# Branch B of a hybrid encoder layer: half of the weights' lower parts and the fourths' sums move to GpSimd, PSUM banks come from three pools, two steps begin later

## The chip, the cores and the metric

The kernel runs on one core of a Trainium2 chip, with TensorE (PE, with its weight loads PEld), VectorE (DVE), ScalarE (ACT), GpSimd (POOL) and SyncE (SP). The metric is the device time of one execution in microseconds (us); lower is better. Every time is of the whole kernel unless a part is named.

## The reference, cut to what matters

One layer, 512 tokens, D = 2048, float32. Both branches and the merge; the change touches branch B and the start of the product with w_out.

```python
h = rmsnorm(x, g_pre)
qkv, z_a, b_raw, a_raw, glu_in, z_b, gate_logits = split(h @ w_in)
y_a = (rmsnorm(gated_delta(conv4(qkv))) * silu(z_a)) @ w_br_a          # branch A
u = causal_depthwise_conv(glu(glu_in), w_dw) + b_dw                    # branch B, 31 taps
u = silu(layernorm(u, ln_g, ln_b)) * silu(z_b)
y_b = u @ w_br_b
gate_a, gate_b = split(sigmoid(gate_logits + b_gate))
x = x + rmsnorm((gate_a * y_a + gate_b * y_b) @ w_out, g_post)
x = x + rmsnorm(sigmoid(x @ w_ple_gate) * (p @ w_ple_proj), g_ple)
```

## The kernel before

**Precision.** A float32 product is made of three matmuls on parts of shorter mantissa: x = xh + xl, w = wh + wl, and x w is xh wh + xl wh + xh wl. Each weight block of 128 x 512 is loaded (two blocks in one transfer, `raw`), its higher part `w[:, 0:T]` is a cast on ScalarE (L126), its lower part a subtraction raw - higher (L127) on the engine that `low_part[0]` names, VectorE at first. The two parts lie in a ring of four buffers `w`; `next_piece()` keeps up to three blocks prepared ahead. A block serves six matmuls in branch B (two row blocks t, three each).

**Order of the work.** A deque `jobs` holds the products in order. Each matmul calls `tick()`, which lets side generators (the normalisation `norm`, `mix`) run on between the matmuls; a `yield n` there waits n ticks. A scheduler then fixes an order for each engine; `pin(...)` keeps an instruction at the place where it was issued. So each engine works through a fixed queue, and an instruction that waits holds up all behind it.

**Normalisation of branch B** (`layer_norm`, L1187 to L1263), while branch A's last products run: load the 16 blocks `ur`; the sum over the channels by a matmul with ones (`sum_ps`, L1200) from `acc`, which GpSimd accumulates (L977); subtract the mean (L1207), squares (L1209, ScalarE) and their sum (L1211, VectorE); reciprocal root `rst` on GpSimd (L1219), spread by a matmul into `rstd_ps` (L1227, PSUM); then per block times rstd (L1231, one input in PSUM), silu (ScalarE), times silu(z_b) (L1236), and the split into higher and lower part `uh`, `ul` (L1245 to L1248).

**Branch B's product** (L1370 to L1497) is done by a Winograd-like scheme on quarters: seven products on sums of quarters for each column half jp (0, 1). The sums of the activations are S1 to S4 (L1262, each on 128 x 256 in float32, then split by `sw_split`: cast on ScalarE, `opl` on VectorE, L1305); S4 takes up S2's buffers. The sums of the weights were made before and lie in memory. In the order of the jobs: P1, P2, Q4 for both column halves (96 matmuls each), then for each half Q5, P6, P7, P3 (48 each). A product's results lie in four (or two) PSUM banks from `b_bank()`, always of the pool `yps` with four banks; branch A's end uses the same pool, and `gt<-yp` (L1158) empties it there. After a product come VectorE's combinations: `snap_b` copies (L1429, ScalarE), `tt_b` sums and differences (L1433), and `fin_b`, which multiplies by the gate (L1291) and adds to `mixed` = `gt` (L1294). P7 ends two column blocks and P2 and P3 one, so a burst of 15 VectorE operations follows P7 of the first half (jp 0), two of them reading PSUM (`yp`).

**From branch B to w_out.** `mix` (`split_mixed`) turns the finished `mixed` by transposes on TensorE (`turned`, `tp`, L1318) and makes the operands of the next product, also in quarters: `combine_low` for the first half of the columns, `combine_high` (four steps, with splits and sums on VectorE, L1305, L1349 to L1357) for the other. It runs beside P3 and the second half. The product with w_out begins with P1, P7, P1, P7; its weights are blocks of 128 x 1024 (`wsp`, higher part L1553, lower part L1554 on VectorE); its banks `f` come from `bank()`: two of `ups`, four of `fps`, two of `gps`, and round again.

Of the kernel before, what the change touches and what calls it, by code (L numbers as in the profile page):

```python
# [81 lines left out]
def _body(ctx, tc, A, out):  # L82
# [28 lines left out]

    prep_src = deque()
    prepped = deque()
    low_part = [nc.vector]

    def prep():
        if not prep_src:
            return
        src = prep_src.popleft()
        raw = rawp.tile([P, 1024], F32, tag="raw", name="raw", bufs=3)  # L120
        nc.sync.dma_start(raw, src)
        for q in range(2):
            rq = raw[:, q * T:(q + 1) * T]
            w = ring.tile([P, 1024], F32R, tag="w", name="w")
            hi, lo = w[:, 0:T], w[:, T:]
            nc.scalar.copy(hi, rq)  # L126
            low_part[0].tensor_tensor(lo, rq, hi.bitcast(F32), ALU.subtract)  # L127
            hi_lo[id(hi)] = w.rearrange("p (s c) -> p s c", s=2)
            prepped.append((hi, lo))

# [29 lines left out]
    def run_jobs():  # L160
        while jobs:
            jobs.popleft()()
# [833 lines left out]
    def convs():  # L996
        ready = last = None
        while scanning[0] < NH // 2 - 1:
            yield 4
        while len(done) < NK:  # L1000
            ready = ready or near()
            if not ready:
                if last and len(taken) == NK:
                    filtered(*last)
                    last = None
                yield 1
                continue
            (i, u, y), ready = ready, None
            w0 = V_DW + i * TAPS
            for s in range(1, TAPS):  # L1010
                pin(nc.vector.scalar_tensor_tensor(y[:, s:], u[:, 0:T - s], vv(w0 + TAPS - 1 - s), y[:, s:], ALU.mult, ALU.add))  # L1011
                if s == 28 and last:
                    filtered(*last)
                    last = None
                if s == 24:
                    ready = near()
                yield pace(s)
            nc.sync.dma_start(u_dram[i], y)
            last = i, y
            if ups and not taken_ps[0]:  # L1020
                taken_ps[0] = True
                low_part[0] = nc.gpsimd

    def side_convs():
        for _ in range(SIDE):
# [161 lines left out]
    def hp(name):  # L1187
        return hpool.tile([P, T], F32, tag="h", name=name)

    def layer_norm():  # L1190
        for i in range(NK):
            while i not in done:
                yield
            u_t[i] = hp("ur")
            nc.sync.dma_start(u_t[i], u_dram[i])
            yield 1
        low_part[0] = nc.vector
        yield 8
        pm = ups.tile([P, T], F32, tag="u", name="sum_ps")
        pin(mm(pm, ones, acc[0], start=True, stop=True))  # L1200
        mean = ups.tile([P, T], F32, tag="u", name="mean_ps")
        nc.scalar.activation(mean, pm, AF.Copy, scale=1.0 / D)
        acc2 = hp("acc2")
        yield 6
        for i in range(NK):
            u = u_t[i]
            pin(nc.vector.tensor_tensor(u, u, mean, ALU.subtract))  # L1207
            sq = hp("lsq") if i else acc2
            nc.scalar.activation(sq, u, AF.Square)  # L1209
            if i:  # L1210
                pin(nc.vector.tensor_tensor(acc2, acc2, sq, ALU.add))  # L1211
            yield 7
        pvr = ups.tile([P, T], F32, tag="u", name="var_ps")
        for tt in range(NTT):
            mm(pvr[:, tt:tt + 1], acc2[:, tt * P:(tt + 1) * P], ones[:, 0:1], start=True, stop=True)
        var = lnp.tile([P, NTT], F32, name="var")
        nc.vector.tensor_scalar(var, pvr[:, 0:NTT], 1.0 / D, EPS, ALU.mult, ALU.add)
        rst = lnp.tile([P, NTT], F32, name="rst")
        nc.gpsimd.tensor_tensor(rst, var, mhalf_c[:, 0:NTT], ALU.pow)  # L1219
        dg = hp("dg")  # L1220
        for tt in range(NTT):
            nc.vector.tensor_scalar(dg[:, tt * P:(tt + 1) * P], ident, rst[:, tt:tt + 1], None, ALU.mult)
        for i in range(3):
            load_zb(i)
        yield 22
        rstd = ups.tile([P, T], F32, tag="u", name="rstd_ps")
        pin(mm(rstd, ones, dg, start=True, stop=True))  # L1227
        yield 6
        for i in range(NK):
            u = u_t[i]  # L1230
            pin(nc.vector.tensor_tensor(u, u, rstd, ALU.mult))  # L1231
            nc.scalar.activation(u, u, AF.Silu, scale=vv(V_LNG + i), bias=vv(V_LNB + i))
            yield 6
            if i + 3 < NK:
                load_zb(i + 3)
            nc.vector.tensor_tensor(u, u, zb[i], ALU.mult)  # L1236
            if i < 8:
                if i % 2 == 0:
                    ua[i // 2] = low(0, "uh"), low(0, "ul")
                c = slice((i % 2) * 256, (i % 2) * 256 + 256)  # L1240
                uh, ul = [x[:, c] for x in ua[i // 2]]
                nc.scalar.copy(uh, u[:, LO])
                nc.vector.tensor_tensor(ul, u[:, LO], uh.bitcast(F32), ALU.subtract)
            else:
                uh, ul = low(0, "uh"), low(LOP if i == NK - 1 else 0, "ul")  # L1245
                nc.scalar.copy(uh, u)
                nc.vector.tensor_tensor(ul, u, uh.bitcast(F32), ALU.subtract)
            uT[i] = (uh, ul)  # L1248
            yield 6
        us1, us3 = [None] * 4, [None] * 4  # L1250
        for name in ("S1", "S2", "S3", "S4"):
            for k2 in range(4):
                if name == "S1":
                    us1[k2] = hp("usf")
                elif name == "S3":
                    us3[k2] = hp("usf")
                t = us3[k2] if name == "S3" else us1[k2]
                for kk, c in halves(k2):
                    u, v = u_t[kk], u_t[kk + 8]
                    a, b, op = {"S1": (u[:, HI], v[:, HI], ALU.subtract), "S2": (t[:, c], u[:, LO], ALU.subtract),  # L1260
                                "S3": (u[:, LO], u[:, HI], ALU.subtract), "S4": (t[:, c], v[:, LO], ALU.add)}[name]
                    nc.vector.tensor_tensor(t[:, c], a, b, op)  # L1262
                yield 4  # L1263
                uS[name][k2] = sw_split(*((s2, "s2") if name == "S1" else (hpool, "h") if name == "S3" else (lop, "lop")), t)
                yield 6

    def load_zb(i):
        zb[i] = hp("zb")
# [45 lines left out]
    def turned(kk):  # L1314
        ps = gps.tile([P, T], F32, tag="g", name="tp")
        for tt in range(NTT):
            c = (kk % 4) * P
            nc.tensor.transpose(ps[:, tt * P:(tt + 1) * P], mixed[tt][kk // 4][:, c:c + P], ident)  # L1318
        return ps

    def combine_low(k2):
        while added[k2 // 2] < NTT:
            yield
        ah = hpool.tile([P, T], F32R, tag="h", name="ah")
        al = hpool.tile([P, T], F32R, tag="h", name="al")
        s3_ = hpool.tile([P, T], F32, tag="h", name="sf")
        for kk, c in halves(k2):
            ps = turned(kk)
            yield 2
            cm[kk] = slots.tile([P, T], F32, tag="s", name="cm")  # L1330
            nc.scalar.copy(cm[kk], ps)
            nc.scalar.copy(ah[:, c], cm[kk][:, LO])
            nc.vector.tensor_tensor(al[:, c], cm[kk][:, LO], ah[:, c].bitcast(F32), ALU.subtract)
            nc.vector.tensor_tensor(s3_[:, c], cm[kk][:, LO], cm[kk][:, HI], ALU.subtract)
            yield
        AW["A11"][k2] = (ah, al)
        Sf[k2] = s3_

    def combine_high(k2):
        while added[k2 // 2 + 2] < NTT:  # L1340
            yield
        two = [turned(kk + 8) for kk, _ in halves(k2)]
        yield 2
# [46 lines left out]
        return [x[:, c:c + P] for x in uS[name][kk // 2]]  # L1390

    b_banks = [0]

    def b_bank():
        b_banks[0] += 1
        return yps.tile([P, T], F32, tag="y", name="yp")

    def b_job(products, done_, gates=()):
# [37 lines left out]
    def branch_b():  # L1436
# [40 lines left out]
        b_job([(0, "P1"), (1, "P1")], p1, [(S2_, LOW, 0), (S2_, LOW, 2)])  # L1477
        b_job([(0, "P2"), (1, "P2")], p2)
        b_job([(0, "Q4"), (1, "Q4")], q4)
        jobs.append(lambda: finish("norm"))  # L1480
        for jp in range(2):
            b_job([(jp, "Q5")], q5(jp))
            b_job([(jp, "P6")], p6(jp), [(LO_, HIGH, 2 * jp + 1), (LO_, HIGH, 2 * jp)])
# [7 lines left out]
    lnp_ctx = ExitStack()  # L1491
    lnp = lnp_ctx.enter_context(tc.tile_pool(name="lnp", bufs=1))
    run_jobs()
    lnp_ctx.close()
    s2_ctx.close()

# [77 lines left out]
            mm(ps, lh, wl[:, c], start=False, stop=kk == 7)  # L1574

    banks = [-1]

    def bank():
        banks[0] += 1
        if banks[0] % 8 < 2:  # L1580
            return ups.tile([P, T], F32, tag="u", name="f")
        if banks[0] % 8 < 6:
            return fps.tile([P, T], F32, tag="f", name="f")
        return gps.tile([P, T], F32, tag="g", name="f")

# [313 lines left out]
```

## Time and profile before

| | us |
|---|---|
| median of 3 runs | 2441.02 (2440.77 to 2441.69) |
| the profiled execution | 2441.21 |
| its span | 2439.4 |
| TensorE busy | 2399.4 |
| VectorE busy | 1877.9 |
| ScalarE busy | 1206.9 |
| GpSimd busy | 496.5 |

Times in the trace count from the span's start; the profiled execution takes 1.8 us more than its span. The normalisation's mean falls at about 1833 (L1200), its reciprocal root at 1869 (L1227), P1 begins at about 1900, P7 of the first half ends near 2014, the product with w_out begins near 2091. A row of the timeline is: start, time of the row, engine, line, operation, out<-in, shapes, x how many; in brackets the idle time before it and what ended that. Several like instructions in a run make one row, and since instructions overlap at their ends, n of them take less than n times the time of one.

### The profile page before, as it was taken

How to read it: one execution, taken by the hardware profiler on the slowest of the kernel's cores; microseconds unless marked ns; L12 is line 12 of the kernel's file. 1: busy time of each engine (PE TensorE's matmuls, PEld its weight loads, DVE VectorE, ACT ScalarE, POOL GpSimd, SP SyncE). 2: the span in 40 equal slices, each digit the busy share in tenths (PEclk: the TensorE clock that was granted, in tenths of full speed). 3: DMA queues.
4: the chain of work that ended last, by engine and by line, in shares of the span. 5: the costliest groups of instructions: out<-in, count | busy, mean ns of one | idle time of the engine just before them, and what ended most of it. 6: DMA issues, size and time to landing. Idle time of an engine off the chain costs nothing. (4 is left out here: it accounts for less than half of the span.)

```text
span 2439.4 us, 33786 instructions
## 1 busy us (share of the span) xinstructions
PE 2399.4 (98%) x11870; PEld 1972.0 (81%) x11870; DVE 1877.9 (77%) x3500; ACT 1206.9 (49%) x2409; POOL 496.5 (20%) x513
## 2 busy tenths in 40 slices
PE   9999999999999999999999999999999899999998
PEld 7888888887788888888888887888887687787886
DVE  8878878776778677776868778999998868867644
ACT  6455545554554545445454544544325554644532
POOL 1001110011112112111212213998730000000000
PEclk9999999999999999999999999999999999999999
DMA  7576776664366565556565453533534465764652
GB/s 273 171 201 189 212 200 206 202 164 167 131 173 185 165 186 144 189 151 173 153 193 173 130 170 94 160 128 105 179 116 164 147 207 182 258 204 146 211 175 76
DMA packets 142234, 417.96 MB, mean 171 GB/s; under 512 B 16240, under 2 KB 24688, under 8 KB 141040
## 3 DMA queue, kind: packets, MB, share of 16 engines
q1 hardware_dynamic: 120304, 327.71, 39.8%
q0 software_dynamic: 19456, 83.90, 14.9%
q10 hardware_dynamic: 2304, 4.20, 0.5%
q8 instruction: 93, 1.52, 0.2%
q14 instruction: 77, 0.63, 0.1%
HBM read 384.28 MB, written 98.57 MB: 198 GB/s over the span
## 5 line engine op out<-in xcount | busy, mean ns | idle before, releaser
L126 ACT CAST w<-raw 128x512 fp32r<-128x512 f32 x628 | 385.9, 618 | 495.9 <-PE g L187 261.5
L185 PE MATMUL g<-hl,w 128*128 128x512 f32 x1536 | 610.5, 397 | 0.0
L187 PE MATMUL g<-hh,w 128*128 128x512 f32 x1536 | 608.2, 396 | 0.0
L183 PE MATMUL g<-hh,w 128*128 128x512 f32 x1536 | 608.1, 396 | 0.0
L127 DVE TENSOR_TENSOR w<-raw,w 128x512 fp32r<-128x512 f32 x514 | 355.1, 698 | 148.6 <-ACT w L126 146.3
L185 PEld LDWEIGHTS g<-hl,w 128*128 128x128 f32 x1536 | 289.0, 188 | 55.4 <-issue 1.4
L183 PEld LDWEIGHTS g<-hh,w 128*128 128x128 f32 x1536 | 289.2, 188 | 54.1
L187 PEld LDWEIGHTS g<-hh,w 128*128 128x128 f32 x1536 | 289.1, 188 | 54.0 <-POOL w L127 0.3
L1011 DVE SCALAR_TENSOR_TENSOR uc<-up,vec,uc 128x497 f32<-128x497 f32 (+29 forms) x390 | 282.3, 734 | 13.2 <-ACT uc L990 1.9
L127 POOL TENSOR_TENSOR w<-raw,w 128x512 fp32r<-128x512 f32 x114 | 146.6, 1299 | 58.0 <-ACT w L126 57.6
L710 DVE SCALAR_TENSOR_TENSOR cv<-g,vec,cv 128x511 f32<-128x511 f32 x144 | 106.6, 740 | 41.1 <-ACT cv L708 40.8
L1149 PE MATMUL yp<-w,oh 128*128 128x512 f32 x256 | 100.1, 391 | 0.0
L1151 PE MATMUL yp<-w,ol 128*128 128x512 f32 x256 | 99.5, 391 | 0.0
L1147 PE MATMUL yp<-w,oh 128*128 128x512 f32 x256 | 99.1, 389 | 0.0
L898 DVE TENSOR_TENSOR prod<-UT,VT 128x2 f32<-128x2 f32 (+30 forms) x248 | 87.2, 352 | 6.5
L1516 POOL TENSOR_TENSOR rmsm<-totm,mhalf_c 128x2 f32<-128x2 f32 x2 | 2.1, 1040 | 386.2 <-DVE totm L1514 386.2
L1033 POOL TENSOR_TENSOR uc<-uc,pr 128x511 f32<-128x511 f32 (+29 forms) x60 | 75.9, 1265 | 8.3 <-ACT pr L1032 7.7
L1748 PE MATMUL f<-w,xh 128*128 128x512 f32 x192 | 75.1, 393 | 1.0 <-DVE xl L1669 1.0
L1749 PE MATMUL f<-w,xh 128*128 128x512 f32 x192 | 75.1, 391 | 0.3 <-DVE w L127 0.3
L1573 PE MATMUL f<-wsp,opl 128*128 128x512 f32 x192 | 75.3, 392 | 0.0
L1572 PE MATMUL f<-wsp,oph 128*128 128x512 f32 x192 | 75.1, 391 | 0.0
L1750 PE MATMUL f<-w,xl 128*128 128x512 f32 x192 | 74.9, 390 | 0.0
(424 smaller groups left out, 5029.9 us busy)
## 6 DMA issues: line engine op xcount, KB each, us to landing
raw<-in_w_in SPq DMA_DIRECT2D x194, 512.0 KB, 3.4
wb_sums<-in_w_br_b POOLq DMA_DIRECT2D x48, 512.0 KB, 7.3
wo_sums<-in_w_out POOLq DMA_DIRECT2D x48, 512.0 KB, 8.0
raw<-in_w_ple_gate SPq DMA_DIRECT2D x40, 512.0 KB, 4.0
raw<-in_w_br_a SPq DMA_DIRECT2D x32, 512.0 KB, 3.4
raw<-wb_sums SPq DMA_DIRECT2D x32, 512.0 KB, 3.9
raw<-in_w_ga SPq DMA_DIRECT2D x24, 512.0 KB, 4.8
raw<-in_w_gb SPq DMA_DIRECT2D x24, 512.0 KB, 4.8
```

Of the source, the lines that this page charges most:

```text
L126: nc.scalar.copy(hi, rq)
L127: low_part[0].tensor_tensor(lo, rq, hi.bitcast(F32), ALU.subtract)
L183: mm(ps, wh, rh, start=(k == 0), stop=False)
L185: mm(ps, wh, rl, start=False, stop=False)
L187: mm(ps, wl, rh, start=False, stop=(k == NK - 1))
L710: nc.vector.scalar_tensor_tensor(y[:, s:], ps[:, 0:T - s], vv(w0 + 3 - s), y[:, s:], ALU.mult, ALU.add)
L898: pin(nc.vector.tensor_tensor(pv_, um, vm, ALU.mult))
L1011: pin(nc.vector.scalar_tensor_tensor(y[:, s:], u[:, 0:T - s], vv(w0 + TAPS - 1 - s), y[:, s:], ALU.mult, ALU.add))
L1033: pin(nc.gpsimd.tensor_tensor(y[:, s:], y[:, s:], pr[:, s:], ALU.add))
L1147: mm(ps[tt], lh[:, b], wh, start=k == 0, stop=False)
L1149: mm(ps[tt], lh[:, b], wl, start=False, stop=False)
L1151: mm(ps[tt], ll[:, b], wh, start=False, stop=k == NK - 1)
```

## The change

- `low_part` becomes a list of two, for the two blocks of a transfer. In the convolution's time both are GpSimd, as before. The normalisation no longer gives them back to VectorE at its start but in its mean loop at i = 11; after `rst` the first of the two goes to GpSimd again, to the end of branch B. So from `rst` on every second lower part is made on GpSimd (60 of 120).
- The sums S1 to S4 (32 operations on 128 x 256) move from VectorE to GpSimd, with 7 and 7 ticks behind each instead of 4 and 6; S4 begins only when Q4 is done; the call that finished the normalisation ahead of Q5 is gone.
- `b_bank()`: of the products, counted by `b_banks // 2` (two banks each), number 0 and 4 (P1 and Q4 of the first half) take their banks from `gps`, 3, 7 and 10 (P2 of the second half, P6 of the first, Q5 of the second) from `ups`, the others from `yps`.
- The first transpose of each `turned` is pinned. `combine_low` waits 24 ticks before its first block; `combine_high` does not begin until branch B's jobs have all run (`ending`).
- The final stage's banks come in another order: `ffffuuffuuffffgg`, then round by eights.

The lines move a little: L1219 becomes L1220, L1231 L1233, L1262 L1266, L1291 and L1294 L1295 and L1298, L1305 L1309, L1318 L1322, L1433 L1447, L1554 L1569.

GpSimd's order from the reciprocal root on. Before, it holds nothing more of branch B after it; `rmsm` belongs to the norm after w_out:

```order
L977 TENSOR_TENSOR acc<-acc,uc 128x512
L127 TENSOR_TENSOR w<-raw,w 128x512 x7
L977 TENSOR_TENSOR acc<-acc,uc 128x512 x2
L1219 TENSOR_TENSOR rst<-var,mhalf_c 128x4
L1516 TENSOR_TENSOR rmsm_20387<-totm_20384,mhalf_c 128x2
```

Now (`w` is a lower part, `usf` a sum of quarters, its inputs `ur` the normalised blocks):

```order
L977 TENSOR_TENSOR acc<-acc,uc 128x512
L127 TENSOR_TENSOR w<-raw,w 128x512 x5
L1220 TENSOR_TENSOR rst<-var,mhalf_c 128x4
L127 TENSOR_TENSOR w<-raw,w 128x512 x3
L1266 TENSOR_TENSOR usf<-ur 128x256
L127 TENSOR_TENSOR w<-raw,w 128x512
L1266 TENSOR_TENSOR usf<-ur 128x256 x2
L127 TENSOR_TENSOR w<-raw,w 128x512
L1266 TENSOR_TENSOR usf<-ur 128x256 x3
L127 TENSOR_TENSOR w<-raw,w 128x512
L1266 TENSOR_TENSOR usf<-ur 128x256 x3
L127 TENSOR_TENSOR w<-raw,w 128x512
```

So lower parts and sums stand in turn in a queue that was empty; 60 lower parts and 32 sums follow `rst`, and lower parts stand ahead of the last accumulation of the mean (L977) as of `rst` itself.

VectorE's order at the end of P7 of the first half. Before (`bsnap` are the copies of earlier products, `bd` a difference kept for P3, `gt` the mixed rows):

```order
L127 TENSOR_TENSOR w<-raw,w 128x512 x8
L1433 TENSOR_TENSOR bsnap<-yp,bsnap 128x512
L127 TENSOR_TENSOR w<-raw,w 128x512
L1433 TENSOR_TENSOR bsnap<-bsnap 128x512 x2
L1291 TENSOR_TENSOR bsnap<-bsnap,gb 128x512 x2
L1433 TENSOR_TENSOR bd<-bsnap 128x512
L1294 TENSOR_TENSOR gt<-gt,bsnap 128x512
L1433 TENSOR_TENSOR bsnap<-yp,bsnap 128x512
L1294 TENSOR_TENSOR gt<-gt,bsnap 128x512
L1433 TENSOR_TENSOR bsnap<-bsnap 128x512 x2
L1291 TENSOR_TENSOR bsnap<-bsnap,gb 128x512 x2
L1294 TENSOR_TENSOR gt<-gt,bsnap 128x512 x2
```

and now:

```order
L127 TENSOR_TENSOR w<-raw,w 128x512 x4
L1447 TENSOR_TENSOR bsnap<-yp,bsnap 128x512
L1447 TENSOR_TENSOR bsnap<-bsnap 128x512 x2
L1295 TENSOR_TENSOR bsnap<-bsnap,gb 128x512 x2
L1447 TENSOR_TENSOR bd<-bsnap 128x512
L1298 TENSOR_TENSOR gt<-gt,bsnap 128x512
L1447 TENSOR_TENSOR bsnap<-yp,bsnap 128x512
L1298 TENSOR_TENSOR gt<-gt,bsnap 128x512
L1447 TENSOR_TENSOR bsnap<-bsnap 128x512 x2
L1295 TENSOR_TENSOR bsnap<-bsnap,gb 128x512 x2
L1298 TENSOR_TENSOR gt<-gt,bsnap 128x512 x2
L127 TENSOR_TENSOR w<-raw,w 128x512 x4
```

The 15 operations are the same, but no lower part of VectorE's stands among them any more, and half as many stand ahead of them, since the others are in GpSimd's queue.

VectorE's order where the last stage opens, before (`wsp` are lower parts of w_out's blocks, `opl`, `sf` the splits and sums of `combine_high`, `bd` P3's end):

```order
L1305 TENSOR_TENSOR opl<-tp,oph 128x512 x2
L127 TENSOR_TENSOR w<-raw,w 128x512
L1349 TENSOR_TENSOR sf<-cm,tp 128x256 x2
L127 TENSOR_TENSOR w<-raw,w 128x512 x2
L1305 TENSOR_TENSOR opl<-sf,oph 128x512
L1554 TENSOR_TENSOR wsp<-raw,wsp 128x1024
L1353 TENSOR_TENSOR sf<-sf,cm 128x256 x2
L1433 TENSOR_TENSOR bd<-yp,bd 128x512 x2
```

and now:

```order
L127 TENSOR_TENSOR w<-raw,w 128x512 x3
L1569 TENSOR_TENSOR wsp<-raw,wsp 128x1024
L1447 TENSOR_TENSOR bd<-yp,bd 128x512 x2
L1295 TENSOR_TENSOR bd<-bd,gb 128x512 x2
L1298 TENSOR_TENSOR gt<-gt,bd 128x512 x2
L1569 TENSOR_TENSOR wsp<-raw,wsp 128x1024 x2
L1309 TENSOR_TENSOR opl<-sf,oph 128x512 x3
L1569 TENSOR_TENSOR wsp<-rw,wsp 128x1024
```

Here the whole of `combine_high` has moved behind P3's end, and three `wsp` come ahead of its first operation on VectorE (its splits of `tp` come later still).

```diff
@@ -111,7 +111,7 @@
 
     prep_src = deque()
     prepped = deque()
-    low_part = [nc.vector]
+    low_part = [nc.vector, nc.vector]
 
     def prep():
         if not prep_src:
@@ -124,7 +124,7 @@
             w = ring.tile([P, 1024], F32R, tag="w", name="w")
             hi, lo = w[:, 0:T], w[:, T:]
             nc.scalar.copy(hi, rq)
-            low_part[0].tensor_tensor(lo, rq, hi.bitcast(F32), ALU.subtract)
+            low_part[q].tensor_tensor(lo, rq, hi.bitcast(F32), ALU.subtract)
             hi_lo[id(hi)] = w.rearrange("p (s c) -> p s c", s=2)
             prepped.append((hi, lo))
 
@@ -1019,7 +1019,7 @@
             last = i, y
             if ups and not taken_ps[0]:
                 taken_ps[0] = True
-                low_part[0] = nc.gpsimd
+                low_part[:] = [nc.gpsimd] * 2
 
     def side_convs():
         for _ in range(SIDE):
@@ -1194,7 +1194,6 @@
             u_t[i] = hp("ur")
             nc.sync.dma_start(u_t[i], u_dram[i])
             yield 1
-        low_part[0] = nc.vector
         yield 8
         pm = ups.tile([P, T], F32, tag="u", name="sum_ps")
         pin(mm(pm, ones, acc[0], start=True, stop=True))
@@ -1209,6 +1208,8 @@
             nc.scalar.activation(sq, u, AF.Square)
             if i:
                 pin(nc.vector.tensor_tensor(acc2, acc2, sq, ALU.add))
+            if i == 11:
+                low_part[:] = [nc.vector] * 2
             yield 7
         pvr = ups.tile([P, T], F32, tag="u", name="var_ps")
         for tt in range(NTT):
@@ -1217,6 +1218,7 @@
         nc.vector.tensor_scalar(var, pvr[:, 0:NTT], 1.0 / D, EPS, ALU.mult, ALU.add)
         rst = lnp.tile([P, NTT], F32, name="rst")
         nc.gpsimd.tensor_tensor(rst, var, mhalf_c[:, 0:NTT], ALU.pow)
+        low_part[0] = nc.gpsimd
         dg = hp("dg")
         for tt in range(NTT):
             nc.vector.tensor_scalar(dg[:, tt * P:(tt + 1) * P], ident, rst[:, tt:tt + 1], None, ALU.mult)
@@ -1249,6 +1251,8 @@
             yield 6
         us1, us3 = [None] * 4, [None] * 4
         for name in ("S1", "S2", "S3", "S4"):
+            while name == "S4" and not b_u[0].get("s4"):
+                yield 4
             for k2 in range(4):
                 if name == "S1":
                     us1[k2] = hp("usf")
@@ -1259,10 +1263,10 @@
                     u, v = u_t[kk], u_t[kk + 8]
                     a, b, op = {"S1": (u[:, HI], v[:, HI], ALU.subtract), "S2": (t[:, c], u[:, LO], ALU.subtract),
                                 "S3": (u[:, LO], u[:, HI], ALU.subtract), "S4": (t[:, c], v[:, LO], ALU.add)}[name]
-                    nc.vector.tensor_tensor(t[:, c], a, b, op)
-                yield 4
+                    nc.gpsimd.tensor_tensor(t[:, c], a, b, op)
+                yield 7
                 uS[name][k2] = sw_split(*((s2, "s2") if name == "S1" else (hpool, "h") if name == "S3" else (lop, "lop")), t)
-                yield 6
+                yield 7
 
     def load_zb(i):
         zb[i] = hp("zb")
@@ -1315,12 +1319,16 @@
         ps = gps.tile([P, T], F32, tag="g", name="tp")
         for tt in range(NTT):
             c = (kk % 4) * P
-            nc.tensor.transpose(ps[:, tt * P:(tt + 1) * P], mixed[tt][kk // 4][:, c:c + P], ident)
+            turn = nc.tensor.transpose(ps[:, tt * P:(tt + 1) * P], mixed[tt][kk // 4][:, c:c + P], ident)
+            if tt == 0:
+                pin(turn)
         return ps
 
     def combine_low(k2):
         while added[k2 // 2] < NTT:
             yield
+        if k2 == 0:
+            yield 24
         ah = hpool.tile([P, T], F32R, tag="h", name="ah")
         al = hpool.tile([P, T], F32R, tag="h", name="al")
         s3_ = hpool.tile([P, T], F32, tag="h", name="sf")
@@ -1337,7 +1345,7 @@
         Sf[k2] = s3_
 
     def combine_high(k2):
-        while added[k2 // 2 + 2] < NTT:
+        while not ending:
             yield
         two = [turned(kk + 8) for kk, _ in halves(k2)]
         yield 2
@@ -1390,9 +1398,15 @@
         return [x[:, c:c + P] for x in uS[name][kk // 2]]
 
     b_banks = [0]
+    ending = []
 
     def b_bank():
+        n = b_banks[0] // 2
         b_banks[0] += 1
+        if n in (3, 7, 10):
+            return ups.tile([P, T], F32, tag="u", name="yp")
+        if n in (0, 4):
+            return gps.tile([P, T], F32, tag="g", name="yp")
         return yps.tile([P, T], F32, tag="y", name="yp")
 
     def b_job(products, done_, gates=()):
@@ -1477,7 +1491,6 @@
         b_job([(0, "P1"), (1, "P1")], p1, [(S2_, LOW, 0), (S2_, LOW, 2)])
         b_job([(0, "P2"), (1, "P2")], p2)
         b_job([(0, "Q4"), (1, "Q4")], q4)
-        jobs.append(lambda: finish("norm"))
         for jp in range(2):
             b_job([(jp, "Q5")], q5(jp))
             b_job([(jp, "P6")], p6(jp), [(LO_, HIGH, 2 * jp + 1), (LO_, HIGH, 2 * jp)])
@@ -1491,6 +1504,8 @@
     lnp_ctx = ExitStack()
     lnp = lnp_ctx.enter_context(tc.tile_pool(name="lnp", bufs=1))
     run_jobs()
+    ending.append(True)
+    low_part[:] = [nc.vector] * 2
     lnp_ctx.close()
     s2_ctx.close()
 
@@ -1574,12 +1589,15 @@
             mm(ps, lh, wl[:, c], start=False, stop=kk == 7)
 
     banks = [-1]
+    order = "ffffuuffuuffffgg"
 
     def bank():
         banks[0] += 1
-        if banks[0] % 8 < 2:
+        n = banks[0]
+        kind = order[n] if n < 16 else order[8 + n % 8]
+        if kind == "u":
             return ups.tile([P, T], F32, tag="u", name="f")
-        if banks[0] % 8 < 6:
+        if kind == "f":
             return fps.tile([P, T], F32, tag="f", name="f")
         return gps.tile([P, T], F32, tag="g", name="f")
 
```

## The prediction

> **What bounds the kernel now.** I read the page's head first, then the windows around branch B, then the waits of TensorE there.
>
> ```profile
> span 2439.4 us, 33786 instructions
> PE 2399.4 (98%) x11870; PEld 1972.0 (81%) x11870; DVE 1877.9 (77%) x3500; ACT 1206.9 (49%) x2409; POOL 496.5 (20%) x513
> ```
>
> TensorE is busy 98% of the span, so the kernel ends when TensorE's work ends, and the change can only win or lose what TensorE idles (or runs at a lower clock) in the stretch that it touches. The windows show where that is; the columns are busy time of PE, PEld, DVE, ACT and POOL, each with its instructions, then the granted clock and the DMA.
>
> ```profile
> core 0: us, PE busy (x) PEld busy (x) DVE busy (x) ACT busy (x) POOL busy (x), PEclk, DMA share, GB/s
> 1800.00:1860.00 60.00, 59.57 (x261) 48.65 (x260) 50.06 (x79) 21.51 (x37) 7.72 (x6) 1.00 0.32 106
> 1860.00:1885.00 25.00, 24.22 (x108) 19.28 (x107) 20.55 (x39) 14.35 (x24) 1.04 (x1) 1.00 0.78 273
> 1885.00:1938.00 53.00, 43.61 (x173) 33.67 (x172) 52.20 (x102) 34.54 (x60) 0.00 (x0) 0.94 0.42 139
> 1938.00:2010.00 72.00, 71.21 (x315) 58.70 (x315) 45.90 (x71) 37.30 (x62) 0.00 (x0) 1.00 0.59 197
> 2010.00:2030.00 20.00, 16.78 (x68) 13.16 (x67) 16.84 (x30) 8.22 (x15) 0.00 (x0) 0.91 0.49 159
> 2070.00:2100.00 30.00, 23.17 (x91) 17.99 (x90) 29.25 (x48) 14.94 (x22) 0.00 (x0) 0.89 0.50 180
> ```
>
> At full supply a matmul takes 71.21/315 = 0.226 us. By that price 1885 to 1938 holds 173 x 0.226 = 39.1 us of work: 13.9 us are lost, and VectorE is busy 52.20 of 53. From 2010 to 2030, 20 - 68 x 0.226 = 4.6 us are lost, from 2070 to 2100 30 - 91 x 0.226 = 9.4. These three stretches, 28 us together, are what VectorE costs; in the 72 us between 1938 and 2010 it has 26 us to spare. GpSimd does nothing after 1885. The waits name what TensorE stood for (us in total, times, longest):
>
> ```profile
> PE tp L1318 <- DVE gt L1294: 6.0, 3, 3.2
> PE yp L1415 <- ACT bsnap L1429: 4.1, 1, 4.1
> PE f L1574 <- DVE wsp L1554: 4.0, 1, 4.0
> PE yp L1419 <- DVE w L127: 3.6, 4, 1.5
> PE yp L1415 <- DVE gt L1158: 2.5, 1, 2.5
> PE sum_ps L1200 <- POOL acc L977: 0.4, 1, 0.4
> ```
>
> **What the moved work costs, and what two engines do to each other.** The next rows are a run of GpSimd's lower parts, its lower parts and its 256-wide sums as groups, and VectorE's same two operations back to back.
>
> ```profile
> 1513.08 2.54 POOL L127 TENSOR_TENSOR w<-raw,w 128x512 fp32r<-128x512 f32 x2
> L127 POOL TENSOR_TENSOR w<-raw,w 128x512 fp32r<-128x512 f32 x114 | 146.6, 1299 | 58.0 <-ACT w L126 57.6
> L837 POOL TENSOR_TENSOR E<-E,c_all 128x256 f32<-128x256 f32 x16 | 9.8, 610 | 0.0
> 2023.48 2.48 DVE L127 TENSOR_TENSOR w<-raw,w 128x512 fp32r<-128x512 f32 x4
> 1934.64 2.76 DVE L1262 TENSOR_TENSOR usf<-usf,ur 128x256 f32<-128x256 f32 x8
> ```
>
> GpSimd takes 1.25 us per lower part in a run (2.54 for two, with the tail) and 0.61 per 256-wide sum; VectorE takes 0.60 ((2.48 - 0.68)/3) and 0.34. So GpSimd is about half as fast. Whether that is free depends on rows where both work:
>
> ```profile
> 587.47 1.33 POOL L683 TENSOR_TENSOR tg<-cst,gl 128x512 fp32r<-128x512 f32 x1 [5.09 <-PE r_ps L688]
> 587.79 1.55 DVE L127 TENSOR_TENSOR w<-raw,w 128x512 fp32r<-128x512 f32 x1
> 1499.22 6.51 DVE L1011 SCALAR_TENSOR_TENSOR uc<-sg,vec,uc 128x487 f32<-128x487 f32 x6
> 1501.22 1.40 POOL L127 TENSOR_TENSOR w<-raw,w 128x512 fp32r<-128x512 f32 x1 [13.15 <-ACT w L126]
> 1503.93 1.29 POOL L127 TENSOR_TENSOR w<-raw,w 128x512 fp32r<-128x512 f32 x1 [1.32 <-ACT w L126]
> 581.04 1.33 POOL L683 TENSOR_TENSOR tg<-cst,gl 128x512 fp32r<-128x512 f32 x1 [5.29 <-PE r_ps L688]
> 581.37 0.69 DVE L692 TENSOR_TENSOR E_mk<-r_ps,gc 128x512 f32<-128x512 f32 x1
> ```
>
> The lower part at 587.79 took 1.55 instead of 0.69: it came while GpSimd ran from 587.47 to 588.80, and the excess 0.86 is near the 1.0 that GpSimd still had to go. Six operations at 1499.22, 3.9 us of work at 0.65 each, took 6.51 with two GpSimd lower parts (2 x 1.25 = 2.5) inside: 3.9 + 2.5 = 6.4. But the one at 581.37, which reads PSUM (r_ps), took its normal 0.69 beside GpSimd. So an operation of VectorE with both inputs in SBUF stands still for as long as GpSimd works, and one with a PSUM input does not. The Trainium skill, page "SBUF — State Buffer", section "SBUF: two separate sides", calls the shared port pair "an **exclusive lock**, not a bandwidth split"; these rows agree, and it speaks against this change. Most operations of branch B on VectorE (lower parts, fourths' splits, L1291, L1294, the subtractions of L1433) have both inputs in SBUF: a lower part moved to GpSimd frees 0.60 us of VectorE and takes 1.25 from it wherever VectorE has a queue.
>
> **The sum, part by part** (plus is slower; the base is the profiled run's 2441.21 us, of which 2439.4 are span; the median of the runs is 0.2 less).
>
> 1. Mean. GpSimd keeps the lower parts to i = 11. The last accumulation (L977) stands behind up to one weight, 1.25 us, for which L1200 waits (0.4 today), and the squares' additions on VectorE, both inputs in SBUF, are held up; against that, VectorE loses lower parts and has 60 - 50.06 = 9.9 us to spare in that window. +1.5, bounds 0 and +3.
>
> 2. From the reciprocal root (rst) to Q4's weights. Today's loss is the 13.9 us of 1885 to 1938, two waits among it: a bank that L1158 must free first, and a bank that P1's copy frees.
>
> ```profile
> 1900.72 0.39 PE L1419 MATMUL yp<-w,uh 128*128 128x512 f32 x1
> 1903.64 0.50 PE L1415 MATMUL yp<-w,uh 128*128 128x512 f32 x1 [2.53 <-DVE gt L1158]
> 1904.95 0.63 PE L1417 MATMUL yp<-w,ul 128*128 128x512 f32 x1
> 1905.38 0.63 PE L1419 MATMUL yp<-w,uh 128*128 128x512 f32 x1
> 1934.11 0.50 PE L1415 MATMUL yp<-w,uh 128*128 128x512 f32 x1 [4.05 <-ACT bsnap L1429]
> ```
>
> Banks from three pools take both waits away, and with each the slow matmuls behind it: after the wait of 2.53 the pitch is 0.43 (1904.95 to 1905.38), nearly twice 0.226, for some eight matmuls, 1.7 us. (The Trainium skill, "TensorE: Matmul & The Clock Gate", section "What's actually happening", has the clock halved after an idle window of about 3.4 us; by that the shorter wait would cost 2.5 and not 4.2. The row has the clock halved after 2.53, and the row decides.) But taking a wait away gains nothing where the weights are late next. Up to the end of the sums and some 22 weights of branch B, TensorE has about 275 matmuls, 62.2 us. In the new order of GpSimd there stand 16 lower parts and 32 sums: 16 x 1.25 + 32 x 0.61 = 39.5. VectorE keeps 48 operations of 0.60 and 8 of 0.34 with both inputs in SBUF (31.5), and 20 that read PSUM (12.0). The first two groups exclude each other: 39.5 + 31.5 = 71.0 if all PSUM readers lie beside GpSimd, 83.0 if none do. Most of those readers are the 16 multiplications by rstd_ps, and in GpSimd's order only three weights stand ahead of the first sum, so I take the serial end less 3.8: 79.2 - 62.2 = 17 lost, and 3 for the slow clock: 20, so +6 against 13.9. Bounds: 8.8 less 13.9 is -5, and 20.8 + 3 less 13.9 is +10.
>
> 3. P2's twelve operations. Eight of them have both inputs in SBUF; about two GpSimd weights (2.5) come between, and the next lower part of VectorE stands behind all. L127 is waited for 1.5 at worst today. +2, bounds 0 and +3.
>
> 4. P7 of the first half. Rows of today: its first operation, its last ones, and TensorE's wait.
>
> ```profile
> 2013.69 0.68 DVE L1433 TENSOR_TENSOR bsnap<-yp,bsnap 128x512 f32<-128x512 f32 x1
> 2022.27 1.28 DVE L1294 TENSOR_TENSOR gt<-gt,bsnap 128x512 f32<-128x512 f32 x2
> 2023.61 0.56 PE L1318 MATMUL tp<-cst,gt 128*128 128x128 f32 x2 [3.17 <-DVE gt L1294]
> ```
>
> Call the end of P7 E (about 2013.6). Today one lower part stands inside the burst and four follow at 2023.48, 9.9 us after E; TensorE loses 4.6 in all, clock included. The transposes that wait now go later (the 24 yields), but that frees nothing: TensorE then waits for the lower part behind the same burst. In the new order none of VectorE's lower parts stands inside. Three weights are ready at E, so the fourth's lower part is needed at E + 3 x 6 x 0.226 + 2 x 0.226 = E + 4.5. The 15 operations take 9.0, the lower part 0.6, and GpSimd puts two or three of its own between, 2.5 to 3.8, 13 operations having both inputs in SBUF: about E + 12.3. Lost 7.8 and 2 of slow clock, 9.8, so +5. Without any hold it is 5.1 + 1.8, +2. Bounds +2 and +6.
>
> 5. P7 of the second half. Today 9.4 less the 4.0 and 1 of point 7, 4.4. The same burst, with both PSUM readers at its head (1.2 us hidden): +4, bounds +1.4 and +5. P3 of the first half comes with six operations, four of them held once: +0.5, 0 to +1.
>
> 6. Q4, Q5, P6 cost nothing either way: the 315 matmuls of 1938 to 2010 are 52 weights, 26 of them on GpSimd, 26 x 1.25 = 33 us of holds against 26 us of spare VectorE time and the 26 x 0.60 = 16 that it is rid of. Without that cover some of the 33 would be lost.
>
> 7. The opening of the last stage. Today one wait:
>
> ```profile
> 2091.44 0.50 PE L1574 MATMUL f<-wsp,ah 128*128 128x512 f32 x1 [3.96 <-DVE wsp L1554]
> ```
>
> The lower part of wsp stood behind the high half's splits and sums; now that half begins only when branch B has ended, behind the first wsp. I take 4 off, bounds -5.4 (with all the slow clock) and -1 (the splits are wanted by the same products, a little later).
>
> Sum: 1.5 + 6 + 2 + 5 + 4 + 0.5 - 4 = +15, so 2441.21 + 15 = 2456.
>
> **Rivals.** *A, the waits go and nothing takes their place.* GpSimd's work falls beside PSUM readers and into VectorE's idle time. Then the two bank waits with their clock (-4.2 and about -2 of the second, since weights are late there too), the opening (-4), the mean (+1) and the P7 bursts (+2, +1.4, both without a hold) and +1.4 for P2 give -4.4: 2437; with all of P7's loss gone too it would be about 2428. For it: 26 us of idle VectorE, and the PSUM reader at 581.37. Against: VectorE's 52.20 of 53 in the very stretch where the sums go. It decides if the hold in point 2 stays under some 5 us of the 20. *B, the two cancel.* Point 2 at -2 and the bursts at +2 each, opening -4: about 2441. *C, GpSimd itself becomes the bound.* If a 256-wide sum costs it what a 512-wide operation does (1.30, not 0.61), 32 x 0.69 = 22 us more stand in its queue ahead of weights, of which some 14 cannot hide in point 2: about 2470. Against: the row of L837.
>
> **How the numbers follow.** Forecast 0.62, C 0.10, A 0.15, B 0.13. A difference under 0.2%, 4.9 us, can hardly be told from none: A (2428 to 2437) is faster, B is the same, the forecast and C are slower, so 0.15, 0.13 and 0.72. All bounds at once would span 2434 to 2468; low 2438 takes in B and half of A, high 2470 C's value. The forecast's own range is 2447 to 2466.
>
> **What would show it.** Right: groups of VectorE's L127 and L1309 whose mean rises from 0.69 towards 1; TensorE waiting for POOL w L127 and DVE w L127 around P1, P2 and behind both P7, 5 to 10 us each; no wait of a first matmul of P1 or P2 for a bank; no wait of the first f for wsp; GpSimd busy some 95 us more (60 x 1.25 + 32 x 0.61). Wrong: VectorE's L127 stays at 0.69 with GpSimd beside it, or TensorE's loss from 1885 to 1938 shrinks below 10 us, or the loss behind P7 stays at 4.6; then the time is at or below 2441.

## The result, and the profile after

The changed kernel takes 2463.26 us (median of 5 runs, 2461.33 to 2464.51), the kernel before 2441.10 (5 runs, 2440.77 to 2442.80): a ratio of 1.0088, with a 95% interval of 1.0073 to 1.0102. It is 22 us slower. The forecast was 2456 with a range of 2438 to 2470.

The head of the changed kernel's page:

```profile
span 2461.5 us, 33863 instructions
PE 2405.2 (98%) x11870; PEld 1973.4 (80%) x11870; DVE 1860.9 (76%) x3396; ACT 1207.1 (49%) x2409; POOL 627.3 (25%) x617
```

Over the whole span, GpSimd's lower parts are 186 now (114 in the row quoted of before):

```profile
L127 POOL TENSOR_TENSOR w<-raw,w 128x512 fp32r<-128x512 f32 x186 | 246.4, 1334 | 185.8 <-ACT w L126 181.4 <-DMA raw<-wb_sums 2.5 <-DMA raw<-in_w_br_b 1.4
```

So 72 lower parts (60 behind the reciprocal root in GpSimd's queue, 12 ahead of it) and 32 sums left VectorE, at 0.60 and 0.34 us 54 us of work; yet its busy time fell by 17 only (1877.9 to 1860.9). GpSimd's rose by 131 (496.5 to 627.3), where 72 x 1.25 + 32 x 0.61 would be 110. Both engines were slower at the same work. The groups between 1800 and 2115 us show which operations (line, engine, operation, shapes, count; busy us, mean ns; idle before):

```profile
L127 DVE TENSOR_TENSOR w<-raw,w 128x512 fp32r<-128x512 f32 x68 | 57.2, 850 | 53.4 <-ACT w L126 53.3
L1309 DVE TENSOR_TENSOR opl<-usf,oph 128x512 fp32r<-128x512 f32 x16 | 16.8, 1063 | 9.8 <-ACT oph L1307 9.6
L1249 DVE TENSOR_TENSOR ul<-ur,uh 128x512 fp32r<-128x512 f32 x8 | 8.6, 1077 | 0.0
L1233 DVE TENSOR_TENSOR ur<-ur,rstd_ps 128x512 f32<-128x512 f32 x16 | 10.2, 677 | 0.6 <-PE rstd_ps L1229 0.6
L1158 DVE TENSOR_TENSOR gt<-yp,gt 128x512 f32<-128x512 f32 x12 | 8.0, 681 | 3.1 <-PE yp L1151 3.1
```

The first three have both inputs in SBUF: 0.850, 1.063 and 1.077 us in place of 0.688, 0.683 and 0.684 in the kernel before. The last two read PSUM (`rstd_ps`, `yp`) and keep 0.68. GpSimd in the same stretch:

```profile
L127 POOL TENSOR_TENSOR w<-raw,w 128x512 fp32r<-128x512 f32 x76 | 104.8, 1380 | 133.6 <-ACT w L126 129.5 <-DMA raw<-wb_sums 2.5 <-DMA raw<-in_w_br_b 1.4
L1266 POOL TENSOR_TENSOR usf<-ur 128x256 f32<-128x256 f32 x16 | 15.9, 1018 | 7.7 <-DVE ur L1238 7.7
```

A 256-wide sum took 1.02 us here; the 256-wide operation that the prediction quotes took 0.61. TensorE's waits from 1470 to 2160:

```profile
PE yp L1433 <- DVE w L127: 17.6, 6, 6.3
PE yp L1433 <- POOL w L127: 8.7, 5, 3.1
PE f L1587 <- ACT snap L1619: 5.7, 1, 5.7
PE sum_ps L1199 <- POOL acc L977: 1.3, 1, 1.3
PE yp L1429 <- DVE gt L1158: 0.6, 1, 0.6
```

Of before's waits, those of the transposes (6.0), for `bsnap` (4.1) and for `wsp` (4.0) are gone and the one behind L1158 shrank from 2.5 to 0.6; the waits for lower parts rose from 3.6 to 26.3, and one for `snap` is new.

Places that both programs have, by the start of the operation named in each timeline (us from the span's start), show where the 22 us came in:

| place | before | after | difference | added in the step |
|---|---|---|---|---|
| first matmul of P1 | 1899.59 | 1901.54 | +1.95 | +1.95 |
| VectorE reads P2 | 1955.02 | 1962.54 | +7.52 | +5.57 |
| VectorE reads P7, first half | 2013.69 | 2023.45 | +9.76 | +2.24 |
| VectorE reads P3, first half | 2030.00 | 2042.91 | +12.91 | +3.15 |
| VectorE reads P7, second half | 2066.29 | 2080.23 | +13.94 | +1.03 |
| VectorE reads P3, second half | 2082.34 | 2100.26 | +17.92 | +3.98 |
| first matmul on `xl`, w_out's product done | 2250.20 | 2272.00 | +21.80 | +3.88 |
| end of the span | 2439.4 | 2461.5 | +22.1 | +0.3 |

The burst behind P7 of the first half in the changed kernel: VectorE, GpSimd beside it, and TensorE.

```profile
2023.45 0.69 DVE L1447 TENSOR_TENSOR bsnap<-yp,bsnap 128x512 f32<-128x512 f32 x1 [0.69 <-PE yp L1433]
2024.17 1.78 DVE L1447 TENSOR_TENSOR bsnap<-bsnap 128x512 f32<-128x512 f32 x2
2025.88 2.39 DVE L1295 TENSOR_TENSOR bsnap<-bsnap,gb 128x512 f32<-128x512 f32 x2
...
2032.27 1.28 DVE L1295 TENSOR_TENSOR bsnap<-bsnap,gb 128x512 f32<-128x512 f32 x2
2033.47 1.28 DVE L1298 TENSOR_TENSOR gt<-gt,bsnap 128x512 f32<-128x512 f32 x2
2034.68 1.28 DVE L127 TENSOR_TENSOR w<-raw,w 128x512 fp32r<-128x512 f32 x2
```
```profile
2023.51 1.30 POOL L127 TENSOR_TENSOR w<-raw,w 128x512 fp32r<-128x512 f32 x1 [1.42 <-ACT w L126]
2026.23 1.49 POOL L127 TENSOR_TENSOR w<-raw,w 128x512 fp32r<-128x512 f32 x1 [1.42 <-DMA raw<-in_w_br_b]
2028.95 1.65 POOL L127 TENSOR_TENSOR w<-raw,w 128x512 fp32r<-128x512 f32 x1 [1.23 <-ACT w L126]
```
```profile
2028.69 0.39 PE L1431 MATMUL yp<-w,opl 128*128 128x512 f32 x1
2035.41 1.22 PE L1433 MATMUL yp<-w,oph 128*128 128x512 f32 x2 [6.34 <-DVE w L127]
2036.43 0.63 PE L1429 MATMUL yp<-w,oph 128*128 128x512 f32 x1
2036.86 0.63 PE L1431 MATMUL yp<-w,opl 128*128 128x512 f32 x1
```

The two multiplications at 2025.88 take 2.39 instead of 1.28 while GpSimd works from 2026.23 to 2027.72. TensorE runs for 5.6 us on what is ready (to 2029.08), then stands 6.34 us for the lower part behind the burst, and goes on at a pitch of 0.43 for a while.

### The profile page after: what moved, and what is told of

The parts are those of the page before. It is cut to its first block, busy times and chain, and to the rows that moved or that the text cites. A ratio compares the mean times of both kernels' runs of the same rounds, so it can differ in the third digit from the quotient of the medians.

```text
span 2461.5 us, 33863 instructions
## 1 busy us (share of the span) xinstructions
PE 2405.2 (98%) x11870; PEld 1973.4 (80%) x11870; DVE 1860.9 (76%) x3396; ACT 1207.1 (49%) x2409; POOL 627.3 (25%) x617
## 5 line engine op out<-in xcount | busy, mean ns | idle before, releaser
L127 DVE TENSOR_TENSOR w<-raw,w 128x512 fp32r<-128x512 f32 x442 | 318.1, 725 | 158.7 <-ACT w L126 156.6
L127 POOL TENSOR_TENSOR w<-raw,w 128x512 fp32r<-128x512 f32 x186 | 246.4, 1334 | 185.8 <-ACT w L126 181.4
L721 POOL COPY kq<-kc 128x512 f32<-128x512 f32 x16 | 11.5, 722 | 306.4 <-ACT kc L719 169.3
L1587 PE MATMUL f<-wsp,oph 128*128 128x512 f32 x192 | 76.0, 396 | 5.7 <-ACT snap L1619 5.7
L1589 PE MATMUL f<-wsp,oph 128*128 128x512 f32 x192 | 75.6, 393 | 0.0
```

What stands on the lines that cost most here:

```text
L127: low_part[q].tensor_tensor(lo, rq, hi.bitcast(F32), ALU.subtract)
L1587: mm(ps, lh, wh[:, c], start=kk == 0, stop=False)
```

## Experiments

Three theories were set against each other: VectorE stands still while GpSimd works on SBUF (the prediction's); GpSimd is only slow and nothing is held; the banks and the later steps are the loss. For the opening of the last stage there are two readings of the new wait for `snap`.

**Taking the moved work back, one piece at a time.** All three kernels are the changed one with one or both of these edits:

```diff
         nc.gpsimd.tensor_tensor(rst, var, mhalf_c[:, 0:NTT], ALU.pow)
-        low_part[0] = nc.gpsimd
...
-                    nc.gpsimd.tensor_tensor(t[:, c], a, b, op)
+                    nc.vector.tensor_tensor(t[:, c], a, b, op)
```

The first edit alone (lower parts on VectorE again):

> The changed kernel, with all lower parts of branch B on VectorE again after the reciprocal root; the sums stay on GpSimd. Theory (VectorE stands still while GpSimd works on SBUF): the mean of VectorE's L127 falls from 0.85 us to about 0.72, TensorE's two waits of 6.3 behind P7 fall to about 5 (the 15 operations without a hold, and no lower part inside), its waits for GpSimd's lower parts (8.7 in all) go; about 2451 us. Rival 1 (GpSimd is only slow, TensorE waits for its parts and nothing is held): the 8.7 go, but VectorE has 36 us more work, the waits behind P7 stay at 6.3 and more: 2455 to 2460. Rival 2 (banks and the later steps are the loss): 2463, no change.

Measured: 2446.97 us (ratio to before 1.0021, interval 1.0012 to 1.0030), VectorE's lower parts at 0.746 us between 1865 and 2115:

```profile
L127 DVE TENSOR_TENSOR w<-raw,w 128x512 fp32r<-128x512 f32 x123 | 89.1, 746 | 34.6 <-ACT w L126 31.9 <-PE yp L1432 1.8
```

The second edit alone (sums on VectorE again):

> The changed kernel with S1 to S4 on VectorE again; every second lower part stays on GpSimd. Theory: 32 holds of 0.6 us go and 32 x 0.34 us of VectorE work come back, in the stretch where VectorE is short: about 2457 us, and the waits behind P7 (6.3 each) stay, since no sums run there. Rival 1 (nothing is held): VectorE has 11 us more work in its fullest stretch, so 2463 to 2470. Rival 2 (banks and later steps): 2463.

Measured: 2454.82 us (1.0052, interval 1.0037 to 1.0067). Both edits:

> The changed kernel with both the lower parts after the reciprocal root and the sums on VectorE; banks, later steps and the mean part stay changed. Theory: what is left is the banks' gain (some 2 to 4 us), the bursts of P7 without a lower part inside (+2 each) and the opening (+3): about 2444 us, VectorE's L127 at 0.69. Rival 1: without the moved work VectorE is full again: about 2441 or a little above, but with L127 at 0.69 in the changed kernel's place too, which its profile already speaks against. Rival 2 (banks and later steps are the loss): above 2455.

Measured: 2439.38 us (0.9990, interval 0.9980 to 0.9999), and VectorE's group is back to its old mean:

```profile
L127 DVE TENSOR_TENSOR w<-raw,w 128x512 fp32r<-128x512 f32 x121 | 81.2, 693 | 33.2 <-ACT w L126 30.6 <-PE yp L1432 1.8
```

From 1885 to 1938 VectorE is as busy in this last run as in the kernel before (52.20 there), yet TensorE does 217 matmuls where it did 173 (columns as in the prediction's windows):

```profile
1885.00:1938.00 53.00, 49.76 (x217) 39.96 (x216) 51.83 (x100) 35.91 (x63) 0.00 (x0) 1.00 0.49 159
```

So the moved work costs 2463.3 - 2439.4 = 24 us, more than the whole loss; the lower parts alone cost 2454.8 - 2439.4 = 15, the sums alone 2447.0 - 2439.4 = 8. The rest of the change together is a small gain, so the theory that blames it falls. The first edit gives 64 lower parts back, the 60 behind the reciprocal root and four that GpSimd took ahead of it. That the kernel is faster with 64 x 0.60 + 32 x 0.34 = 49 us more work on VectorE speaks against the theory that GpSimd is merely slow, but TensorE also waited 8.7 us for GpSimd's own results; the next pair leaves those out.

**GpSimd work that nobody waits for.** The kernel before, with operations on a raw block that both readers have finished with. With the subtractions, no row of TensorE's, VectorE's or ScalarE's order changes; with the memsets, two pairs of neighbours on VectorE and one on ScalarE change places.

```diff
+    extra = []
...
             low_part[0].tensor_tensor(lo, rq, hi.bitcast(F32), ALU.subtract)
+            if extra and q == 0:
+                nc.gpsimd.tensor_tensor(rq, rq, rq, ALU.subtract)
...
+        extra.append(True)
         dg = hp("dg")
...
     run_jobs()
+    extra.clear()
```

> The kernel before with 60 subtractions on 128 x 512 added on GpSimd from the reciprocal root to the end of branch B, one for every second weight, each on a raw block that is no longer needed; nothing of the result changes, no other engine's order changes, and only the next transfer into that block waits for it. Theory (VectorE stands still while GpSimd reads SBUF): 60 x 1.25 us of holds, of which about 20 us fall where VectorE has no time to spare (some 12 in the stretch of P1 and P2, 3 behind each P7): about 2461 us, VectorE's L127 at 0.8 or more. Rival 1 (GpSimd is only slow, and only TensorE's waits for its results cost): 2441, L127 at 0.69.

Measured: 2461.08 us (1.0078, interval 1.0065 to 1.0092). With two `nc.gpsimd.memset(rq, 0.0)` in place of the subtraction:

> The same as the run with 60 added subtractions, but each is two memsets of the same block (0.53 us each by the trace of before), which write SBUF and read nothing. If any GpSimd work on SBUF holds VectorE: about 2457 us, a little under the run with subtractions. If only one that reads SBUF holds it: 2441 to 2443, VectorE's L127 at 0.69.

Measured: 2441.65 us (1.0000, interval 0.9991 to 1.0009). The groups of VectorE and GpSimd, first with subtractions, then with memsets:

```profile
L128 DVE TENSOR_TENSOR w<-raw,w 128x512 fp32r<-128x512 f32 x123 | 95.3, 796 | 36.1 <-ACT w L127 35.4
L130 POOL TENSOR_TENSOR raw<-raw 128x512 f32<-128x512 f32 x61 | 91.4, 1504 | 139.6 <-DVE w L128 108.8 <-issue 24.0 <-ACT oph L1307 6.1
```
```profile
L128 DVE TENSOR_TENSOR w<-raw,w 128x512 fp32r<-128x512 f32 x121 | 81.2, 687 | 38.1 <-ACT w L127 37.6
L130 POOL MEMSET raw<- 128x512 f32 x61 | 32.1, 527 | 147.4 <-DVE w L128 118.4 <-issue 15.6 <-ACT oph L1308 10.8
L131 POOL MEMSET raw<- 128x512 f32 x61 | 32.1, 527 | 3.5
```

64 us of memsets leave VectorE at 0.687 and the time unchanged, although the raw blocks wait for them too. 91 us of subtractions, whose results nobody uses, cost 19 us, nearly as much as the whole change. The contention is shown, and it needs a GpSimd operation that reads SBUF. One thing besides the hold of VectorE is in the 19 us: the hold works the other way round too. In the run with subtractions, GpSimd, VectorE and ScalarE show this:

```profile
1916.81 11.30 POOL L130 TENSOR_TENSOR raw<-raw 128x512 f32<-128x512 f32 x3 [3.32 <-DVE w L128]
```
```profile
1924.46 0.75 DVE L1266 TENSOR_TENSOR usf<-usf,ur 128x256 f32<-128x256 f32 x2
1930.15 1.29 DVE L128 TENSOR_TENSOR w<-raw,w 128x512 fp32r<-128x512 f32 x2 [4.94 <-ACT w L127]
```
```profile
1929.50 1.14 ACT L127 CAST w<-raw 128x512 fp32r<-128x512 f32 x2 [6.06 <-DMA raw<-in_w_br_b]
```

Three subtractions of GpSimd, 3.75 us of work, lasted 11.30 while VectorE's operations ran one behind the other; the next transfer into `raw` landed late, and ScalarE, VectorE and TensorE then stood for the next weight (6.06 and 4.94 here; TensorE's waits for that cast are 7.2 us in two). So some 7 of the 19 us, and the slow matmuls behind these waits, can have come through the starved GpSimd. That the rest came through held VectorE operations is an estimate by what is left; no run parts the two.

**The other parts of the change, each alone.** The banks of three pools on the kernel before (`b_bank()` as in the diff):

> The kernel before with the banks of three pools for branch B alone. Theory: the waits of 2.5 and 4.1 us for banks go, but in that stretch VectorE is the bound, so only part is won: 2437 to 2440. Rival (VectorE bounds the stretch wholly): 2441, the lost time then stands as waits for L127.

Measured: 2436.18 us (0.9977, interval 0.9967 to 0.9986). The waits for `bsnap` and for L1158 are gone; of TensorE's waits for L127 there are now 6.9 us, 3.3 more than before:

```profile
PE yp L1424 <- DVE w L127: 6.9, 6, 2.9
```

The mean part alone, on the kernel before (`low_part[0] = nc.vector` at i = 11 of the mean loop instead of ahead of the mean):

> The kernel before with only the mean part of the change: GpSimd keeps all lower parts to i = 11 of the mean loop. By the prediction +1.5 us (the last accumulation behind a weight, squares' additions held), 2443; rival (VectorE is rid of some 13 lower parts when the stretch of P1 begins, so it starts ahead): up to 3 us faster, 2439. In both the mean of VectorE's squares' additions (L1211) rises above 0.69 us.

Measured: 2439.93 us (0.9992, interval 0.9984 to 1.0001): no difference that can be told from none, at best a small gain. VectorE's squares' additions did not slow down, so that part of both expectations was wrong (first row). In the changed kernel they did (second row): two of the 15 took 1.29 and 1.36 us, beside lower parts on GpSimd.

```profile
L1210 DVE TENSOR_TENSOR acc<-acc,lsq 128x512 f32<-128x512 f32 x15 | 10.3, 688 | 2.6 <-ACT lsq L1208 2.1
L1210 DVE TENSOR_TENSOR acc<-acc,lsq 128x512 f32<-128x512 f32 x15 | 11.6, 772 | 3.9 <-ACT lsq L1208 3.6
```

**The opening of the last stage.** The changed kernel, with `combine_high` begun as before:

```diff
     def combine_high(k2):
-        while not ending:
+        while added[k2 // 2 + 2] < NTT:
```

> The changed kernel with combine_high begun as before, when its column blocks are added. Theory for the opening (the late half puts its casts into ScalarE's queue ahead of the copies that free banks, hence the wait of 5.7 for the copy): that wait goes, the wait of about 4 for wsp comes back: 2460 us, 3 less. Rival (the wait of 5.7 comes from the new order of banks): the wait for the copy stays and the other comes too: 2466.

Measured: 2459.06 us (1.0072, interval 1.0055 to 1.0089), 4.2 less than the changed kernel. The new wait is gone, the old ones are back:

```profile
PE tp L1322 <- DVE gt L1298: 5.0, 1, 5.0
PE f L1589 <- DVE wsp L1569: 3.3, 1, 3.3
```

The intervals of the two kernels' ratios overlap a little, but the traces bear the gain out: from VectorE's reading of P3 in the second half to the first matmul on `xl` this run needs 2268.46 - 2100.82 = 167.64 us, the changed kernel 171.74, the kernel before 167.86. The bank order of the last stage was the same in both, so by itself it isn't the cause. The changed kernel's rows at its new wait (ScalarE, then TensorE) show what is:

```profile
2151.85 0.62 ACT L1307 CAST oph<-sf 128x512 fp32r<-128x512 f32 x1 [0.78 <-DVE sf L1361]
2154.02 0.62 ACT L1307 CAST oph<-sf 128x512 fp32r<-128x512 f32 x1 [1.55 <-DVE sf L1365]
2154.54 1.07 ACT L1619 COPY snap<-f 128x512 f32<-128x512 f32 x2
```
```profile
2155.18 0.79 PE L1587 MATMUL f<-wsp,oph 128*128 128x512 f32 x1 [5.67 <-ACT snap L1619]
2155.77 0.63 PE L1588 MATMUL f<-wsp,opl 128*128 128x512 f32 x1
2156.19 0.63 PE L1589 MATMUL f<-wsp,oph 128*128 128x512 f32 x1
```

The copies that free a bank stand in ScalarE's queue behind the last casts of `combine_high`, and those wait for VectorE's sums, which stand behind splits that wait for ScalarE's casts in turn. With all of the high half in the opening, the end of this chain comes 53 us into the product, where a bank is due.

**What is worth keeping.** All moved work back on VectorE, `combine_high` begun as before:

> The changed kernel with all moved work back on VectorE and combine_high begun as before; left of the change are the banks, the mean part, combine_low's delay and the last stage's bank order. Theory: from the 2439.4 us of the run without moved work the late half's loss of 3 to 4 us goes: 2436. Rival (the late half is better once VectorE isn't held, since it takes VectorE's work out of P3's time): 2441 or more.

Measured: 2435.02 us (0.9971, interval 0.9960 to 0.9981), faster than both kernels of the case, and 4.4 us less than with the late half. The same without the mean part:

> The run with all moved work back and combine_high begun as before, here also without the mean part: GpSimd does nothing new, and what is left is the banks, combine_low's delay, the later sums and the last stage's bank order. If the mean part costs 1.5 us: 2433.5 instead of 2435.0; if it gains 2: 2437. If banks are all that wins, the time is that of the run with banks alone, 2436.

Measured: 2436.45 us (0.9974, interval 0.9963 to 0.9984). These two and the banks alone (2436.18) can't be told apart: the banks are what wins.

## Why the prediction was right, point by point

The direction, the mechanism and the order of size were right: 2463.3 lies in the range, 22 us against a forecast of 15. By its own steps:

- *The hold.* It was read from three places where GpSimd and VectorE met by chance, and it shows over the whole stretch: means of 0.85 to 1.08 us where both inputs lie in SBUF, 0.68 where one lies in PSUM. The pair of runs with idle GpSimd work shows it without any wait for GpSimd's results. The Trainium skill, page "SBUF — State Buffer", section "SBUF: two separate sides", has the lock, for a VectorE operation with two SBUF inputs, only against a GpSimd operation that reads SBUF; the memsets, which only write, agree: 0.687 us and no loss. What the prediction left out is that GpSimd is held too: its busy time rose by 131 us, where the sign of being right said 95; 15 of the difference are the 12 lower parts ahead of the reciprocal root, the other 21 are slower operations.
- *Point 1, the mean, +1.5.* TensorE waited 1.3 us for the last accumulation, as foreseen, and two of the squares' additions were held in the changed kernel, but by lower parts that GpSimd took ahead of the reciprocal root, which the run with the mean part alone leaves on VectorE. P1 began 1.95 us later in the changed kernel, but that can't be put down to this part: among the profiled executions of four kernels without it P1 begins between 1899.30 (the banks alone) and 1902.21 (the last run above). Over its timed runs the part alone shows no loss (in its profiled execution P1 begins 3.8 us later than before's, and 2.1 us of that are left at the end). Whether it costs or wins 2 us stays open.
- *Points 2 and 3, P1 to Q4 and P2's operations, +6 and +2.* Measured +5.57 by P2 and +2.24 more by P7: 7.8 against 8. Counting the operations that exclude each other gave the right size for the changed kernel. But point 2 takes the 13.9 us lost from 1885 to 1938 before the change for VectorE's cost, and that reading was wrong: without moved work TensorE does 217 matmuls there instead of 173, with VectorE just as busy. From P1's first matmul to the first reading of P7 the run without moved work needs 2004.66 - 1900.74 = 103.92 us, before 114.10, the changed kernel 121.91: the banks, the mean part and the new order together win 10 there, and the moved work costs 18. The sum had neither of the two, only their difference. (The banks alone won 5.8 of 2442.0 us, close to the 6.2 that rival A gave them.)
- *Point 4, P7 of the first half, +5.* Measured +3.15. The lower part came at 11.9 us after P7's end (2035.36 by its row) where 12.3 was worked out, but TensorE had work for 5.6 us and not 4.5, and the wait was 6.34 instead of 7.8. Without moved work the same step is 2021.56 - 2004.66 = 16.90 us long against before's 16.31: +0.6, where +2 was put for the burst with no hold.
- *Point 5, P7 of the second half, +4, and P3, +0.5.* Measured +3.98, and +1.03 for the stretch between.
- *Point 6, Q4 to P6 at nothing.* It held: in the changed kernel TensorE waits for nothing between 1973.42 and the burst behind P7. The 2.24 us lie ahead of that, in a wait of 1.85 us for a lower part behind P2's operations (0.79 before) and slow matmuls after it.
- *Point 7, the opening, -4.* This step failed. It took the wait for `wsp` off and priced the late half's delay at next to nothing ("the splits are wanted by the same products, a little later"). Measured +3.88: the wait did go, and one of 5.67 us with its slow matmuls took its place, since the late half put a chain of casts and sums ahead of the copies that free the banks. The term is off by 7.9 us, more than the 6.8 by which the sum fell short (21.8 against 15); the other terms together were 1 us too high.

Of the rivals, A (nothing is held) would have needed the means to stay at 0.69, and B (the two cancel) a time of 2441. C (a 256-wide sum costs 1.3 us) came as near as the forecast, 2470, by a cause that the rows do not bear out: the sums took 1.02 us, but GpSimd's lower parts were slower too (1.38), and a 256-wide operation took 0.61 in the kernel before.

## What to carry to other kernels

An engine that stands idle is no free helper if it shares a path with the full one: here a lower part moved from VectorE to GpSimd freed 0.60 us and ran for 1.38, in which VectorE's operations with both inputs in SBUF could stand still; those with a PSUM input ran beside it undisturbed. When a change has several parts, time them apart: the banks won 5.8 us, the moved work lost 24, and the late half 4. And when a burst of work is put off to remove a wait, look at what stands behind it in each queue at its new place; here it was the copy that frees a bank.

## What the runs showed of the hardware that was not expected

- The hold goes both ways: GpSimd's lower parts took 1.38 us on average in the changed kernel and its 256-wide sums 1.02, and three subtractions lasted 11.30 us beside a VectorE that ran without a break.
- GpSimd's memsets (0.527 us on 128 x 512) do not disturb VectorE at all: 122 of them, 64 us, changed neither its means nor the time.
- TensorE's matmuls ran at a pitch of 0.43 us instead of 0.226 after the long waits shown above, for about eight of them (2155.77 to 2159.12 after the wait of 5.67), so each such wait cost nearly 2 us more than itself: the nine matmuls from 2155.18 to 2159.12 took 3.94 us, at 0.226 they would have taken 2.03. The length of the wait alone does not decide it: in the changed kernel some eight matmuls from 1974.68 on ran at 0.43 soon after a wait of 1.85 us (to 1973.42), and none did after one of 2.17 us (to 1910.91).
